# A decoder step on one core: rows of 1/rms through memory, two channel groups per matmul, and statistics moved 12 products

## The chip, the cores and the metric

The kernel runs on one core of a Trainium2 chip. A core has TensorE (PE, with its weight loads shown apart as PEld), VectorE (DVE), ScalarE (ACT), GpSimd (POOL) and SyncE (SP), which here issues nearly all DMA transfers. Matmul results land in PSUM, in banks of 512 fp32 columns. The metric is device time in microseconds, the median of several runs. Matmuls appear in the profile as passes: an fp32 product shows as two weight loads and two matmuls, a product of operands rounded to fp32r as one of each.

## The reference

One layer of a hybrid decoder, for a prompt of 1024 positions and for 8 samples of 8 new positions each (64 rows). Cut to what matters here:

```
h = RMSNorm(x)                    # x * rsqrt(mean(x*x) + eps) * gain
q, k, v, gmlp_u, gmlp_v, gate_attn, gate_gmlp = split(h @ w_in)
branch A: sliding-window attention with sinks
branch B: gelu(u) * (W_s[g] LN(gelu(v)) + b[g])  in chunks of 128 positions, 6 channel groups g,
          W_s lower-triangular; for a sample only its first 8 x 8 corner
x = x + (sigmoid(gate_a) * (A @ w_a) + sigmoid(gate_g) * (B @ w_b)) @ w_out
x = x + ConvFFN(RMSNorm(x));  final RMSNorm
```

## The kernel before, in words

The 1088 rows are worked on in two groups: group 0 has the 64 sample rows (`s`) and prompt tiles 0 to 3 (576 rows), group 1 prompt tiles 4 to 7 (512). Every large product is made of three fp32r matmuls over high and low halves of both operands (`hh`/`hl`, `w2h`/`w2l`, `wh`/`wl`), which ACT (L40) and DVE (L41) split from the raw fp32.

The first stage runs from the start to about 107 us. `tokens()` makes gmlp_v and v with the rows on the partitions: per tile of 128 rows 8 chunks of the 1024 channels, three products of 256 columns each (L555), into one PSUM bank; `gv_out` (L597) or `v_out` (L570) on ACT scales the result by the row's 1/rms and stores it. Group 0 goes first, with weights gv 0, gv 1, v, gv 2; then group 1 with v, gv 2, gv 0, gv 1, 96 products for each weight. The weights of a block have two buffers, so that those of the last block (gv 1) are split only after the block of gv 2 has freed its buffer.

1/rms is wanted in two layouts. With the rows on partitions, for the scaling above: `rsg[g]` holds the sums of squares over channel chunks, `stats_tok(g)` adds up the partitions by a matmul with a column of ones (L500) and takes root and reciprocal into `rstg[g]`, 128 partitions by one column per tile (L501, L502). And with the rows along the free dimension, the same on all partitions, for the x tiles that later products use: `stats_all(g)` spreads `rstg[g]` by matmuls with the identity (L512) into a bank, which ACT copies over `rsg[g]` (L514). `sums_of` multiplies x by it (L697). The results for group 0 are split into `t` (`t0_job`), those for group 1 are stored to memory (`t1_job`) and loaded later. These jobs run beside the products, one or none after each tile.

Then PE computes q, k, gmlp_u and the gates by a two-level scheme of seven products per pair of weights (L315, group 0 with 288 columns, group 1 with 256), from about 107 us on. Beside it the layer norm of gmlp_v is made and stored (`vnd`), and `mix_samples` at about 329 us mixes the samples' rows: for each of 6 channel groups one product of 64 rows by 64 columns (L824), with a block-diagonal 64 x 64 matrix per group (`wss`, built at L406 to L411 from a load, a mask and a predicated copy). `mix_job` does the prompt's rows (L852). Attention and the branch products follow from about 430 us, the up projection from about 790, the down projection from about 1247 us to the end.

The order of instructions on each engine is not left to a scheduler: `issue_order` walks each engine's list by a table (`ORDER`), a digit saying how many places ahead the next instruction stands. The staging ring `stg` has 4 buffers, the PSUM ring `st` 7 and `mx` one.

Of the kernel before, what the change touches and what calls it, by code (L numbers as in the profile page):

```python
# [6 lines left out]
F32 = mybir.dt.float32  # L7
F32R = mybir.dt.float32r
I32 = mybir.dt.int32
# [6 lines left out]
P = 128  # L16
D = 1024
KD = 8
NS = 64
# [5 lines left out]
NG = 6  # L25
# [9 lines left out]
def layer(tc, a):  # L35
    nc = tc.nc
    V, S, G, PE = nc.vector, nc.scalar, nc.gpsimd, nc.tensor
# [9 lines left out]
    with ExitStack() as top:  # L47
# [20 lines left out]
        ident = cst.tile([P, P], F32, name="c_ident")  # L68
# [274 lines left out]
        def pick(x, place, lo, hi):  # L343
# [5 lines left out]
                       toks=[("s", 0), *((i, NS + P * i) for i in range(4))]),  # L349
# [7 lines left out]
        dr = lambda name, shape, dt=F32: dram.tile(shape, dt, name=name)  # L357
# [5 lines left out]
        sgd = [[dr(f"sg{e}d{c}", [P, T]) for c in range(KD)] for e in range(2)]  # L363
        vd = [dr(f"vd{i}", [P, NKV, P]) for i in range(7)]
        v3d = dr("v3d", [P, 256])
        dvd = [None, *(dr(f"dvd{i}", [P, NKV, P]) for i in range(1, 8))]
        gvd = {name: dr(f"gvd{name}", [P, GW]) for gr in groups for name, _ in gr["toks"]}
        vnd = [dr(f"vnd{gr['g']}", [P, NG, len(gr["toks"]), P]) for gr in groups]
# [12 lines left out]
        with ExitStack() as ph1:  # L381
            c1 = ph1.enter_context(tc.tile_pool(name="c1", bufs=1))
# [8 lines left out]
            def stage(n):  # L391
                return stg.tile([P, 576], F32, name="stg")[:, :n]
# [3 lines left out]
            def load_late():  # L396
                nc.sync.dma_start(ident, a["ident"])
                late["mprev"] = const1("mprev", [P, 1, P], I32)
                late["sinkb"] = const1("sinkb", [P, NH])
                late["sinks"] = const1("sinks", [P, 2])  # L400
                neg = c1.tile([P, 1], F32, name="c_neg")
                V.memset(neg, NEG)
                late["neg"] = neg
                w2 = c1.tile([NS, NG, NS], F32, name="c_wss")
                w2r = stg.tile([P, 576], F32, name="stg")[:NS, :NG * NS]
                nc.sync.dma_start(w2r, a["wss"])  # L406
                m2 = stg.tile([P, 576], F32, name="stg")[:NS, :NG * NS].bitcast(I32)
                nc.sync.dma_start(m2, a["mss"])
                w2f = w2.rearrange("p a b -> p (a b)")
                V.memset(w2f, 0.0)  # L410
                V.copy_predicated(w2f, m2, w2r)  # L411
                late["wss"] = w2
# [78 lines left out]
            def bank():  # L491
                return psa.tile([P, 512], F32, name="st")

            def stats_tok(g, ps=None):
# [5 lines left out]
                    PE.matmul(pt[:, i:i + 1], acc[:, lo:lo + P], ones[:, 0:1], start=True, stop=True)  # L500
                S.activation(rstg[g], pt, AF.Sqrt, bias=eps, scale=1.0 / D)  # L501
                V.reciprocal(rstg[g], rstg[g])  # L502

            def stats_all(g):

                acc, n, toks = rsg[g], groups[g]["n"], groups[g]["toks"]
                for lo, hi in ((0, 320), (320, n)) if g == 0 else ((0, n),):
                    ps = bank()
                    for i, (name, at) in enumerate(toks):
                        m = NS if name == "s" else P  # L510
                        if lo <= at < hi:
                            PE.matmul(ps[:, at - lo:at - lo + m], rstg[g][0:m, i:i + 1].to_broadcast([m, P]),  # L512
                                      ident[0:m, 0:m], start=True, stop=True)
                    S.copy(acc[:, lo:hi], ps[:, 0:hi - lo])  # L514

            pa0, hs0o, th0, xro = ExitStack(), ExitStack(), ExitStack(), ExitStack()
            gvp = pa0.enter_context(tc.tile_pool(name="gvp", bufs=4))
# [156 lines left out]
            jobs = [x_job(k) for k in range(KD)]  # L674
            tokens(0, ("gv", 0, 1), lambda i, ps: gv_out(0, i, 1, ps), jobs, first_out)
            tokens(0, ("v", 0), lambda i, ps: v_out(0, i, ps), jobs)
            stats_all(0)
            tokens(0, ("gv", 0, 2), lambda i, ps: gv_out(0, i, 2, ps), jobs)
            hs0o.close()
            t0h, xr = right(th0, "T0h"), right(xro, "xr")  # L680
# [38 lines left out]
            none = lambda: None  # L719
            jobs = [lambda: x_in(0)] + [x for kk in range(4) for x in (t0_job(kk), none)] + [t1_job(kk) for kk in range(4)]  # L720
            tokens(1, ("v", 1), lambda i, ps: v_out(1, i, ps), jobs, lambda ps: stats_tok(1))
            stats_all(1)
            wide["again"] = True
            W.emit(W.used + 2)
            for p3 in (2, 0, 1):
# [89 lines left out]
            def mix_samples():  # L815

                mp = late["mp"]
                late["sm"] = mp.tile([P, NG, NS], F32, name="sm")
                ps = psa.tile([P, 512], F32, name="mx", bufs=1)
                for c in range(NG):  # L820
                    if c % 3 == 0:
                        v = stage(3 * P)[:NS].rearrange("p (c k) -> p c k", c=3)
                        nc.sync.dma_start(v, vnd[0][0:NS, c:c + 3, 0])
                    PE.matmul(ps[:, NS * c:NS * c + NS], v[:, c % 3], late["wss"][:, c, :], start=True, stop=True)  # L824
# [1100 lines left out]
def issue_order(tc):  # L1925
# [8 lines left out]
    for name, text in ORDER.items():  # L1934
# [20 lines left out]
        "1"  # L1955
    ),
    "Activation": (
        "1.2(4)b..91..1.44..2.11(10)1223..3(4)1..1.1...1.37..1.3..1..133.2.1(5)777cc.b..e1e.2.a3.33.22.4."
        ".39.1(5)66a.5..467(4)3.2.1.95a211..7...56(4)3..831.2.1.314..34(4)21.62..1.3.52.3.4.b.i4449.333.6"
        ".99...9..2..3.4c..li444.83.22.53.26.7..1.3.4.b.i4449.33.26.993.2.11.44..4c..4449e.f3.22.53.268(5"  # L1960
        ")3.4.7.a4.39.8.3.2.5.4..9H49.7.d47.73.7.35.7...4.2.33.7b4.711...6.1.22.44(4)2274ac2...85237221.."
        "2.37.a47.127.6.2.5.4..48..49b7.3.4.5.6...3.4.7.a47.38.74...5.4..48..49b7.3.4.5.6...3.4.6.83.b467"
        ".1.41.2.1.5346521.433..8a11.53.135.3..1..311B1(8)22(6)11.22(5)y(5)O4(5)5(5)1.44(4)1.L(4)1(7)1.1."
        "54(4)N1.44(4)1(5)1...Q(4)1.1.4(5)1.44(4)1.A(6)1(5)1(9)j1.44(5)1..q..H(6)4(5)T54(6)54(4)1.44(6)5S"
        "4(6)54(6)54(6)Q54(6)54(6)54M(6)54(6)54(6)s44..1...54(6)54c(5)1...5.61..61.2515.51.123.22.24.15.1"
        "51.14.51.152.142.24.13..45..7..1173..171.111.11(4)2...11...126.62.24.1..7..1(4)24..1(4)1.4...33."
        "..229.a.bed262..222...44..9.a.bd3...22...46...3.9.a.b3..a.922(4)5.4..9b..bd3...22...46...3.9.a.b"
        "3..a.92(5)5.4..9a..9a3...22421331..b1.3222..11.22..22.8.9bd3...2221571...3.9.a.b3..a.92211..5.4."
        ".9b..bd3...22...46...3.9.a.b3..a.92(5)5.4..9b..bd3...22...46...3.9.9.93..7.622...22..51.5325266."
        "..5(4)1e.793..a.9322...5.4..9b..bd3...22...46...3.9.a.b3..a.92(5)5.4..9b..bd3...22...46...3.9.a."  # L1970
        "b3..a.92(5)5.4..9b..bd3...22...46...3.7.7.7h...5f.1..124.34..111..41525.1(5)1(7)1.1.1.1.1.1.1.1."
        "1..1(4)KK[92]M.[90]L[89]N1MO[85]O.[83][83].[82][82].1(6)5(4)23.3.3.3.3.3.3.3.3.3.3.3.3.3.3.3.3.3"
        ".3.3(9)2j2i4.35e1466a.9.88.71(8)11121..14l13514g62.466aaaaa.91.1.1...1(5)1(5)1...1.1...1"
    ),
    "DVE": (
        "..nn2(6)91..1.44..2.1...1.1(6)123..3(4)1..1.1.1..26.1.31.2..2g.ff2.dd1ck.jj.iii...777cc.bd.c.b2a"
# [17 lines left out]
        ".77.12...11.1..3..11..11(10)21311111...88(4)4a4...a..118.111.11.111...41.1.2(5)2..3.32..1"  # L1994
    ),
    "SP": (
        "(6)1(17)6789(4)7...3.2.a.ach(10)7.e.d.3d.c.1o(5)99.aa...948..625(4)33.23f.e..511(7)1(13)21.5(4)1"
        "(4)11.3..1.OOT1S...TTVV61.1.2..1.13.2..61.1.2..1.13.2..5615...2..232622.12232vv3..vy..2.424...1."
        ".1.3..62.1.2..464.1.1.4191312.411.21.21c.1512125.1..11.11.1a1411.141...59a.8.41251.324..231...24"
        "66214..2fs1z11(5)1(18)1c.1i6p31...2.m2.63(4)2t.2.s63(4)2.m2.fd.aaab.ib.mf(9)eb(5)79.792(4)3a.d7."  # L2000
        "6g.j7.1.j1(4)1321(13)1(5)1.2...2.1.21113.52544..4..244..244..54.3.5731.8c4..1133.8K..I2...22..56"
        "..y333..1112.111l11(7)22222211..1.445221.111444455.4477...4455.4477...455.55883(4)3344...44.44.."
        ".44.66...1551.44...44.44...44.44...44.99...6(6)1...111f12..3333333..1.988...11122(41)122.111(5)1"
        ".a.9999.888l.lmn.no(24)1.1.1...1...1.1.1.1.1.1.1.1"
    ),
    "PE": (
        "(35)222222222222..223322222222..222222222222..222222222222..222222222222..222222222222(20)555555"
        "555555(3516)5555555(10)aaa(19)5(10)aaaa(52)4(176)44(175)33334(26)4(108)8833334(28)44(113)4444444"
        "444(29)4c(4)888(19)444444444(36)8(22)444444(19)88888...55544444cccc(4)8(18)dd4cccc(4)88(12)88888"
        "...444444(6)8(22)d4cccccc(4)8(12)8888...444444(7)g(8)88888888...4444cccccccccccc(4)o(8)gggggggg."  # L2010
        "..4ccckk(4)ggg(8)8888888gg...4ccccc(4)888(10)gggggggg...4cccckkkk(4)gg(8)888888gg...d4cccccc(4)8"
        "88888888888888c...9488888888888888(4)44444444.3333..111(782)666...333(2369)AAAAAAAAAA(38)cc(1210"
        ")AAAAAA(1868)22222222(36)444"
    ),
}

# [9 lines left out]
def layout(np, x_prompt, x_sample, cache_win_k, cache_win_v, state_conv, norm_mix, w_in, sinks,  # L2026
# [35 lines left out]
    ins["wss"] = np.tile(wst[:8, :, :8], (8, 1, 8)).reshape(NS, NG * NS)  # L2062
    same = (u[:, None] // 8 == u[None] // 8) & (u[:, None] % 8 <= u[None] % 8)
    ins["mss"] = np.tile(same.astype(np.int32), (1, NG))
# [43 lines left out]
```

## Time and profile before

| | us |
|---|---|
| median of 3 runs (1488.43 to 1488.82) | 1488.78 |
| the profiled execution | 1488.75 |
| its span, first to last instruction | 1486.6 |
| PE busy | 1477.0 |
| DVE busy | 1181.6 |
| ACT busy | 857.6 |
| POOL busy | 289.6 |

The profiled execution's time is 2.15 us longer than its span. In rows of a timeline the columns are the start in us from the span's beginning, the length, engine, line, operation, result<-inputs, tile shape and count, and in brackets the idle time before and what ended it. In the chain of work the columns are start, length and what ran. A wait's row gives who waited for whom, the total in us, how often, and the longest. A window's row gives its bounds and length, then the busy time of PE, PEld, DVE, ACT and POOL with counts, the granted clock, the DMA engines' share and GB/s.

### The profile page before, as it was taken

How to read it: one execution, taken by the hardware profiler on the slowest of the kernel's cores; microseconds unless marked ns; L12 is line 12 of the kernel's file. 1: busy time of each engine (PE TensorE's matmuls, PEld its weight loads, DVE VectorE, ACT ScalarE, POOL GpSimd, SP SyncE). 2: the span in 40 equal slices, each digit the busy share in tenths (PEclk: the TensorE clock that was granted, in tenths of full speed). 3: DMA queues.
4: the chain of work that ended last, by engine and by line, in shares of the span. 5: the costliest groups of instructions: out<-in, count | busy, mean ns of one | idle time of the engine just before them, and what ended most of it. 6: DMA issues, size and time to landing. Idle time of an engine off the chain costs nothing.

```text
span 1486.6 us, 30008 instructions
## 1 busy us (share of the span) xinstructions
PE 1477.0 (99%) x11454; PEld 1444.1 (97%) x11454; DVE 1181.6 (79%) x1897; ACT 857.6 (58%) x1797; POOL 289.6 (19%) x395
## 2 busy tenths in 40 slices
PE   9999999999999999999999999999999999999998
PEld 8999999999998999998989999999999999999998
DVE  7889877655587887988678898898898888785686
ACT  8657676554466775864444554654565556363463
POOL 3002110010040322310235222332242222000002
PEclk9999999999999999999999999999999999999998
DMA  7787446774779758458977433332332217983454
GB/s 250 237 290 251 166 165 221 232 233 155 239 247 320 223 158 259 135 188 306 335 268 271 131 123 119 124 124 96 118 133 96 110 59 233 345 290 102 112 164 155
DMA packets 133871, 289.24 MB, mean 195 GB/s; under 512 B 15904, under 2 KB 36064, under 8 KB 133728
## 3 DMA queue, kind: packets, MB, share of 16 engines
q1 hardware_dynamic: 133584, 287.32, 58.0%
q8 instruction: 90, 1.47, 0.4%
q14 instruction: 53, 0.43, 0.1%
q10 hardware_dynamic: 144, 0.01, 0.0%
HBM read 198.72 MB, written 90.52 MB: 195 GB/s over the span
## 4 chain that ended last, share of the span: by engine, by line
PE 95%; DVE 1%; ACT 1%; DMA 1%; issue 1%; POOL 0%; SPq 0%; POOLq 0%; DVEq 0%; ACTq 0%
PE st L315 51%; PE mm L240 17%; PE dn L1749 15%; PE st L555 6%; PE sc L1245 2%; PE po L1296 2%; PE pt L1272 1%; PE mx L852 1%; DMA wraw<-wt 0%; DMA wraw<-wpb 0%; DVE wl L41 0%; DVE s L41 0%; PE po L1196 0%; ACT four L1163 0%; POOL x L1825 0%
## 5 line engine op out<-in xcount | busy, mean ns | idle before, releaser
L315 PE MATMUL st<-t,wh 128*128 128x288 f32 x2128 | 427.7, 294 | 0.0
L315 PEld LDWEIGHTS st<-t,wh 128*128 128x128 f32 x2128 | 335.6, 188 | 0.2
L315 PE MATMUL st<-t,wl 128*128 128x288 f32 x1064 | 311.8, 293 | 0.0
L315 PE MATMUL st<-th,wh 128*128 128x256 f32 x1064 | 294.6, 277 | 0.0
L315 PE MATMUL st<-tl,wh 128*128 128x256 f32 x1064 | 294.2, 277 | 0.0
L315 PE MATMUL st<-th,wl 128*128 128x256 f32 x1064 | 293.9, 276 | 0.0
L315 PEld LDWEIGHTS st<-th,wh 128*128 128x128 f32 x1064 | 199.7, 188 | 0.2 <-ACT kn L296 0.2
L315 PEld LDWEIGHTS st<-t,wl 128*128 128x128 f32 x1064 | 199.8, 188 | 0.0
L315 PEld LDWEIGHTS st<-th,wl 128*128 128x128 f32 x1064 | 199.7, 188 | 0.0
L315 PEld LDWEIGHTS st<-tl,wh 128*128 128x128 f32 x1064 | 199.7, 188 | 0.0
L40 ACT CAST wh<-wraw 128x512 fp32r<-128x512 f32 (+2 forms) x188 | 129.2, 700 | 82.7 <-PE st L315 25.5
L1749 PE MATMUL dn<-th,wh 128*128 128x288 f32 (+1 forms) x616 | 176.6, 287 | 0.0
L1749 PE MATMUL dn<-tl,wh 128*128 128x288 f32 (+1 forms) x616 | 176.2, 286 | 0.0
L1749 PE MATMUL dn<-th,wl 128*128 128x288 f32 (+1 forms) x616 | 175.3, 285 | 0.0
L41 DVE TENSOR_TENSOR wl<-wraw,wh 128x512 fp32r<-128x512 f32 (+2 forms) x188 | 148.8, 805 | 25.2 <-ACT wh L40 23.3
L40 ACT CAST wh<-ws 128x512 fp32r<-128x512 f32 x168 | 102.7, 621 | 86.4 <-PE st L315 53.0
L41 DVE TENSOR_TENSOR wl<-ws,wh 128x512 fp32r<-128x512 f32 x168 | 117.2, 708 | 41.7 <-ACT wh L40 41.0
L1749 PEld LDWEIGHTS dn<-th,wl 128*128 128x128 f32 x616 | 115.9, 188 | 0.1
L1749 PEld LDWEIGHTS dn<-tl,wh 128*128 128x128 f32 x616 | 115.6, 188 | 0.1
L1749 PEld LDWEIGHTS dn<-th,wh 128*128 128x128 f32 x616 | 115.6, 188 | 0.1
L41 DVE TENSOR_TENSOR tl<-traw,th 128x544 fp32r<-128x544 f32 (+1 forms) x85 | 61.0, 722 | 22.6 <-ACT th L40 22.4
L40 ACT CAST th<-traw 128x544 fp32r<-128x544 f32 (+1 forms) x85 | 54.5, 643 | 40.5 <-PE dn L1749 27.0
(308 smaller groups left out, 3188.2 us busy)
## 6 DMA issues: line engine op xcount, KB each, us to landing
wraw<-wt SPq DMA_DIRECT2D x137, 512.0 KB
traw<-td SPq DMA_DIRECT2D x77, 272.0 KB
td<-za SPq DMA_DIRECT2D x22, 544.0 KB
q<-qd SPq DMA_DIRECT2D x16, 512.0 KB
upd<-hl SPq DMA_DIRECT2D x14, 512.0 KB
td<-t SPq DMA_DIRECT2D x11, 544.0 KB
wpart<-wt SPq DMA_DIRECT2D x22, 256.0 KB
qd<-q SPq DMA_DIRECT2D x8, 576.0 KB
```

Of the source, the lines that this page charges most:

```text
L40: S.copy(hi, src)
L41: V.tensor_sub(lo, src, hi.bitcast(F32))
L240: PE.matmul(ps[:, lo:lo + c1 - c0], u[:, k, :], v[:, c0:c1], start=(k == 0 and i == 0), stop=(k == nk - 1 and i == 2))
L315: PE.matmul(ps, u[:, kk, :], v, start=first and kk + i == 0, stop=kk == 3 and i == 2, skip_group_check=True)
L555: PE.matmul(ps, u, v[:, k, :], start=k + i == 0, stop=k == KD - 1 and i == len(todo) - 1)
L852: PE.matmul(ps[:, P * i:P * i + P], vn[:, i], late["wst"][:, c, :], start=True, stop=True)
L1245: PE.matmul(ps[:, h, o0:256], q, kst[kv][:, e, k0:cur + P], start=e == 0, stop=e == 1)
L1272: PE.transpose(pt[:, h * P:h * P + P], s[:, h, 0:P], ident)
L1296: PE.matmul(po, v[:, kv, :], t, start=e == 0, stop=last)
L1749: PE.matmul(place(m, e), u[:, m, :], v[:, lo:hi], start=new and i + k == 0 and (e == 0 or m % 2 == 0), stop=i == NU - 1 and k == 2, skip_g ...
```

## The change

Three edits. First, `stats_all` and its calls are gone. At the end of `stats_tok(g)` SP stores `rstg[g]` as one row of 576 or 512 numbers to memory (4-byte pieces; for group 0 the samples' 64 and the prompt's 4 x 128 apart) and loads that row back to all 128 partitions, over `rsg[g]`. Second, `wss` becomes a 128-row matrix: for each pair of channel groups a block matrix with the even group's 64 x 64 in the upper left and the odd one's in the lower right. The even groups' 64 rows of v are loaded into partitions 0 to 63 and the odd groups' into 64 to 127, and three products of 128 rows and 128 columns take the place of six of 64 and 64. The host makes the wider matrix and mask. Third, the order's table moves the second statistics; the tables of ACT and SP change with the instructions that leave or come, those of DVE and POOL do not.

```
+        rsd = [dr(f"rsd{g}", [1, n]) for g, n in ((0, 576), (1, 512))]
...
-                w2 = c1.tile([NS, NG, NS], F32, name="c_wss")
-                w2r = stg.tile([P, 576], F32, name="stg")[:NS, :NG * NS]
+                w2 = c1.tile([P, NG // 2, P], F32, name="c_wss")
+                w2r = stg.tile([P, 576], F32, name="stg")[:, :NG * NS]
...
                 V.reciprocal(rstg[g], rstg[g])
-
-            def stats_all(g):
...
+                if g == 0:
+                    nc.sync.dma_start(rsd[g][0, 0:NS], rstg[g][0:NS, 0])
+                nc.sync.dma_start(rsd[g][0, NS * (1 - g):].rearrange("(i p) -> p i", p=P), rstg[g][:, 1 - g:])
+                nc.sync.dma_start(acc, rsd[g].to_broadcast([P, groups[g]["n"]]))
...
             tokens(0, ("v", 0), lambda i, ps: v_out(0, i, ps), jobs)
-            stats_all(0)
...
             tokens(1, ("v", 1), lambda i, ps: v_out(1, i, ps), jobs, lambda ps: stats_tok(1))
-            stats_all(1)
...
-                for c in range(NG):
-                    if c % 3 == 0:
-                        v = stage(3 * P)[:NS].rearrange("p (c k) -> p c k", c=3)
-                        nc.sync.dma_start(v, vnd[0][0:NS, c:c + 3, 0])
-                    PE.matmul(ps[:, NS * c:NS * c + NS], v[:, c % 3], late["wss"][:, c, :], start=True, stop=True)
+                v = stage(3 * P).rearrange("p (c k) -> p c k", c=3)
+                for r in range(2):
+                    nc.sync.dma_start(v[NS * r:NS * r + NS], vnd[0][0:NS, r::2, 0])
+                for c in range(NG // 2):
+                    PE.matmul(ps[:, P * c:P * c + P], v[:, c], late["wss"][:, c, :], start=True, stop=True)
...
     "PE": (
...
-        "555555(3516)5555555(10)aaa(19)5(10)aaaa(52)4(176)44(175)33334(26)4(108)8833334(28)44(113)4444444"
+        "555555(337)444444444444(3155)5555555(10)aaa(19)5(10)aaaa(52)4(176)44(175)33334(26)4(108)8833334("
```

What that does to the engines' orders, at three places. The rows are in the order of issue, with result<-inputs and the shape; numbers behind names are buffers, and lines after the change are some 7 lower (L555 is L548, L500 is L501). First PE in the block of v for group 1, before: `hl_854` ends the first tile, `hh_573` (chunk 0) begins the second.

```order
L555 MATMUL st<-w2h,hh_853 128x256
L555 MATMUL st<-w2l,hh_853 128x256
L555 MATMUL st<-w2h,hl_854 128x256
L500 MATMUL mx<-c_ones,rs_251 128x1 x4
L555 MATMUL st<-w2h,hh_573 128x256
L555 MATMUL st<-w2l,hh_573 128x256
```

The same place now, from the second product of the second tile (its chunk 0 is `hh_578` and `hl_579`) to the statistics:

```order
L548 MATMUL st<-w2l,hh_578 128x256
L548 MATMUL st<-w2h,hl_579 128x256
L548 MATMUL st<-w2h,hh_614 128x256
L548 MATMUL st<-w2l,hh_614 128x256
L548 MATMUL st<-w2h,hl_615 128x256
L548 MATMUL st<-w2h,hh_651 128x256
L548 MATMUL st<-w2l,hh_651 128x256
L548 MATMUL st<-w2h,hl_652 128x256
L548 MATMUL st<-w2h,hh_688 128x256
L548 MATMUL st<-w2l,hh_688 128x256
L548 MATMUL st<-w2h,hl_689 128x256
L501 MATMUL mx<-c_ones,rs_253 128x1 x4
```

Chunks 0 to 3 of the second tile, twelve products, now stand ahead of the statistics, which have moved from the border of two tiles into the middle of one.

SP at the same time, before: transfers of x, of the stored v tile 3 (`v3d`), and of the split v (`vd`, `dvd`).

```order
L354 DMA x<-xt 128x576 x2
L586 DMA vd_146<-vst 128x512
L586 DMA dvd_153<-vst 128x512
L586 DMA vd_147<-vst 128x512
L354 DMA x<-xt 128x512
L591 DMA vp<-gv 128x256
```

And now:

```order
L354 DMA x<-xt 128x576 x2
L506 DMA rsd_151<-rst_231 128x4x1
L579 DMA vd_146<-vst 128x512
L579 DMA dvd_155<-vst 128x512
L507 DMA rs_253<-rsd_151 128x512
L579 DMA vd_147<-vst 128x512
L354 DMA x<-xt 128x512
```

The store of the second row stands ahead of two v stores, the load that reads it back behind them, ahead of another v store and of loads of x. For group 0 the two stores stand ahead of the first gv stores, and the load, 15 rows later, ahead of the first store of v.

PE at the samples' mixing, before, between products of the two-level scheme:

```order
L315 MATMUL st<-tl_1765,wh 128x256
L315 MATMUL st<-th_1764,wl 128x256
L824 MATMUL mx<-c_wss,stg 128x64 x6
L315 MATMUL st<-t_1193,wh 128x288 x2
L315 MATMUL st<-t_1193,wl 128x288
```

And now:

```order
L815 MATMUL mx<-c_wss,stg 128x128 x3
L315 MATMUL st<-t_1191,wh 128x288 x2
L315 MATMUL st<-t_1191,wl 128x288
L315 MATMUL st<-t_1192,wh 128x288 x2
L315 MATMUL st<-t_1192,wl 128x288
```

The place is the same; six products are three. The spreading (L512, five products at about 48 us and four at about 74) is simply no longer in PE's list.

More of the change, by code (lines that the diff above doesn't have):

```diff
@@ L403, in load_late @@
                 late["neg"] = neg
-                w2 = c1.tile([NS, NG, NS], F32, name="c_wss")
-                w2r = stg.tile([P, 576], F32, name="stg")[:NS, :NG * NS]
+                w2 = c1.tile([P, NG // 2, P], F32, name="c_wss")
+                w2r = stg.tile([P, 576], F32, name="stg")[:, :NG * NS]
                 nc.sync.dma_start(w2r, a["wss"])
-                m2 = stg.tile([P, 576], F32, name="stg")[:NS, :NG * NS].bitcast(I32)
+                m2 = stg.tile([P, 576], F32, name="stg")[:, :NG * NS].bitcast(I32)
                 nc.sync.dma_start(m2, a["mss"])
@@ L502, in stats_tok @@
                 V.reciprocal(rstg[g], rstg[g])
-            def stats_all(g):
[L506 to L514, printed above, removed]
+                if g == 0:
+                    nc.sync.dma_start(rsd[g][0, 0:NS], rstg[g][0:NS, 0])
+                nc.sync.dma_start(rsd[g][0, NS * (1 - g):].rearrange("(i p) -> p i", p=P), rstg[g][:, 1 - g:])
+                nc.sync.dma_start(acc, rsd[g].to_broadcast([P, groups[g]["n"]]))
             pa0, hs0o, th0, xro = ExitStack(), ExitStack(), ExitStack(), ExitStack()
@@ L1957 @@
     "Activation": (
[L1958 to L1972, printed above, removed]
@@ L1973 @@
-        ".3.3(9)2j2i4.35e1466a.9.88.71(8)11121..14l13514g62.466aaaaa.91.1.1...1(5)1(5)1...1.1...1"
+        "1.2(4)b..91..1.44..2.11(10)1223..3(4)1..1.1...1.37..1.3..1..1.2.1(5)777cc.b..d1d.2.93.3.22.4..39"
+        ".1(5)66a.5..467(4)3.2.1.95a211..7...56(4)3..831.2.1.314..34(4)21.62..1.3.52.3.4.b.i4449.333.6.99"
+        "...9..2..3.4c..li444.83.22.53.26.7..1.3.4.b.i4449.33.26.993.2.11.44..4c..4449e.f3.22.53.268(5)3."
+        "4.7.a4.39.8.3.2.5.4..9H49.7.d47.73.7.35.7...4.2.33.7b4.711...6.1.22.44(4)2274ac2...85237221..2.3"
@@ new lines @@
+        "7.a47.127.6.2.5.4..48..49b7.3.4.5.6...3.4.7.a47.38.74...5.4..48..49b7.3.4.5.6...3.4.6.83.b467.1."
+        "41.2.1.5346521.433..8a11.53.135.3..1..311B1(8)22(6)11.22(5)y(5)O4(5)5(5)1.44(4)1.L(4)1(7)1.1.54("
+        "4)N1.44(4)1(5)1...Q(4)1.1.4(5)1.44(4)1.A(6)1(5)1(9)j1.44(5)1..q..H(6)4(5)T54(6)54(4)1.44(6)5S4(6"
+        ")54(6)54(6)Q54(6)54(6)54M(6)54(6)54(6)s44..1...54(6)54c(5)1...5.61..61.2515.51.123.22.24.15.151."
+        "14.51.152.142.24.13..45..7..1173..171.111.11(4)2...11...126.62.24.1..7..1(4)24..1(4)1.4...33...2"
@@ new lines @@
+        "29.a.bed262..222...44..9.a.bd3...22...46...3.9.a.b3..a.922(4)5.4..9b..bd3...22...46...3.9.a.b3.."
+        "a.92(5)5.4..9a..9a3...22421331..b1.3222..11.22..22.8.9bd3...2221571...3.9.a.b3..a.92211..5.4..9b"
+        "..bd3...22...46...3.9.a.b3..a.92(5)5.4..9b..bd3...22...46...3.9.9.93..7.622...22..51.5325266...5"
+        "(4)1e.793..a.9322...5.4..9b..bd3...22...46...3.9.a.b3..a.92(5)5.4..9b..bd3...22...46...3.9.a.b3."
+        ".a.92(5)5.4..9b..bd3...22...46...3.7.7.7h...5f.1..124.34..111..41525.1(5)1(7)1.1.1.1.1.1.1.1.1.."
@@ L1974 @@
+        "1(4)KK[92]M.[90]L[89]N1MO[85]O.[83][83].[82][82].1(6)5(4)23.3.3.3.3.3.3.3.3.3.3.3.3.3.3.3.3.3.3."
+        "3(9)2j2i4.35e1466a.9.88.71(8)11121..14l13514g62.466aaaaa.91.1.1...1(5)1(5)1...1.1...1"
     ),
@@ L1996 @@
     "SP": (
[L1997 to L2004, printed above, removed]
+        "(6)1(17)9abc..111181114131b1bdi(11)7.g.f.3f.e.1q(5)bb2cc.11..948..625(4)33.23f.e..511(7)1(13)21."
+        "5(4)1(4)11.3..1.OOT1S...TTVV61.1.2..1.13.2..61.1.2..1.13.2..5615...2..232622.12232vv3..vy..2.424"
+        "...1..1.3..62.1.2..464.1.1.4191312.411.21.21c.1512125.1..11.11.1a1411.141...59a.8.41251.324..231"
+        "...2466214..2fs1z11(5)1(18)1c.1i6p31...2.m2.63(4)2t.2.s63(4)2.m2.fd.aaab.ib.mf(9)eb(5)79.792(4)3"
+        "a.d7.6g.j7.1.j1(4)1321(13)1(5)1.2...2.1.21113.52544..4..244..244..54.3.5731.8c4..1133.8K..I2...2"
+        "2..56..y333..1112.111l11(7)22222211..1.445221.111444455.4477...4455.4477...455.55883(4)3344...44"
+        ".44...44.66...1551.44...44.44...44.44...44.99...6(6)1...111f12..3333333..1.988...11122(41)122.11"
+        "1(5)1.a.9999.888l.lmn.no(24)1.1.1...1...1.1.1.1.1.1.1.1"
     ),
@@ L2007 @@
         "(35)222222222222..223322222222..222222222222..222222222222..222222222222..222222222222(20)555555"
-        "555555(3516)5555555(10)aaa(19)5(10)aaaa(52)4(176)44(175)33334(26)4(108)8833334(28)44(113)4444444"
[L2009 to L2013, printed above, removed]
+        "555555(337)444444444444(3155)5555555(10)aaa(19)5(10)aaaa(52)4(176)44(175)33334(26)4(108)8833334("
+        "28)44(113)4444444444(29)4c(4)888(19)444444444(36)8(22)444444(19)88888...55544444cccc(4)8(18)dd4c"
+        "ccc(4)88(12)88888...444444(6)8(22)d4cccccc(4)8(12)8888...444444(7)g(8)88888888...4444ccccccccccc"
+        "c(4)o(8)gggggggg...4ccckk(4)ggg(8)8888888gg...4ccccc(4)888(10)gggggggg...4cccckkkk(4)gg(8)888888"
+        "gg...d4cccccc(4)888888888888888c...9488888888888888(4)44444444.3333..111(782)666...333(2369)AAAA"
+        "AAAAAA(38)cc(1210)AAAAAA(1868)22222222(36)444"
     ),
@@ L2061, in layout @@
     ins["wst"] = wst
-    ins["wss"] = np.tile(wst[:8, :, :8], (8, 1, 8)).reshape(NS, NG * NS)
+    wss = np.zeros((2, NS, NG // 2, 2, NS), np.float32)
+    mss = np.zeros(wss.shape, np.int32)
     same = (u[:, None] // 8 == u[None] // 8) & (u[:, None] % 8 <= u[None] % 8)
-    ins["mss"] = np.tile(same.astype(np.int32), (1, NG))
+    for e in range(2):
+        wss[e, :, :, e] = np.tile(wst[:8, :, :8], (8, 1, 8))[:, e::2]
+        mss[e, :, :, e] = same[:, None]
+    ins["wss"], ins["mss"] = (x.reshape(P, NG * NS) for x in (wss, mss))
     ck = cache_win_k[0]
```

## The prediction

> **What bounds the kernel now.** I read the page's shares first, then who TensorE (PE) waited for, then the chain of work that ended last.
>
> ```profile
> span 1486.6 us, 30008 instructions
> PE 1477.0 (99%) x11454; PEld 1444.1 (97%) x11454; DVE 1181.6 (79%) x1897; ACT 857.6 (58%) x1797; POOL 289.6 (19%) x395
> PE 95%; DVE 1%; ACT 1%; DMA 1%; issue 1%; POOL 0%; SPq 0%; POOLq 0%; DVEq 0%; ACTq 0%
> PE sc L1146 <- issue: 1.3, 1, 1.3
> ```
>
> PE is busy 99% of the span and carries 95% of the chain; its longest wait, in attention, is 1.3 us. So a microsecond taken from PE's stream is worth a microsecond, unless the work that feeds PE cannot come earlier. The chain, in order of time (start, length, what), prices the PE work that the change touches:
>
> ```profile
> 25.43 22.35 PE st L555 x196
> 47.78 1.45 PE st L512 x10
> 49.23 15.43 PE st L555 x136
> 64.66 0.79 PE mx L500 x8
> 65.45 8.59 PE st L555 x72
> 74.03 0.89 PE st L512 x8
> 74.92 32.66 PE st L555 x288
> 107.58 221.35 PE st L315 x1788
> ```
>
> From 25 to 329 us the chain is PE's own stream, piece touching piece: nothing else is waited for there. The reader should also see a pace: 136 products in 15.43 us and 288 in 32.66 are 0.1134 us each, but the 72 between the second statistics (L500) and the second spreading (L512) take 8.59, or 0.119.
>
> **The change, part by part.** *Spreading of 1/rms by matmul removed.* The two pieces of L512 go from PE: 1.45 and 0.89 us. What follows them starts that much earlier. Sum so far 2.34. The three ACT copies behind them (L514) go too; ACT is 58% busy and no PE wait names it in this stretch, so I cost them at nothing.
>
> *The mixing of the samples.* Starts on PE's timeline around it, and around a later group of 128-row, 128-column products (L852) for comparison:
>
> ```profile
> 328.66 0.28 PE L315 MATMUL st<-th,wl 128*128 128x256 f32 x1
> 328.87 1.55 PE L824 MATMUL mx<-c_wss,stg 64*128 64x64 f32 x12
> 330.34 0.54 PE L315 MATMUL st<-t,wh 128*128 128x288 f32 x2
> 330.72 0.29 PE L315 MATMUL st<-t,wl 128*128 128x288 f32 x1
> 347.99 0.28 PE L315 MATMUL st<-th,wl 128*128 128x256 f32 x1
> 348.10 1.05 PE L852 MATMUL mx<-wst,vn 128*128 128x128 f32 x8
> 348.91 0.51 PE L315 MATMUL st<-t,wh 128*128 128x288 f32 x2
> 349.26 0.29 PE L315 MATMUL st<-t,wl 128*128 128x288 f32 x1
> ```
>
> Each fp32 product is two passes (six products, x12). From the last product before to the third after, twelve 64-row passes take 330.72 - 328.66 = 2.06 us and eight 128-row passes 349.26 - 347.99 = 1.27. Inside the groups a pass starts every (1.55 - 0.27)/11 = 0.116 us for 64 columns, (1.05 - 0.28)/7 = 0.110 for 128: the column count does not show, and going from 128 to 64 rows costs 0.1 us more at each end (328.66 to 328.87 against 347.99 to 348.10). Three products of 128 rows and columns are six passes: 1.27 - 2 x 0.11 = 1.05. Gain 2.06 - 1.05 = 1.01 us; sum 3.35. The Trainium skill has a rule that speaks against this term: in "TensorE: Matmul & The Clock Gate", section "Back-to-back issue gap", a lone warm matmul's gap is N/2.4 + 2.5 ns, so that two 64-column passes (58 ns) are worth one of 128 (56 ns) and pairing the groups gains nothing; the sum would then be 2.34. The rows above contradict it here, since both widths take 0.11 us.
>
> The two loads of v for it keep their shapes and places in SP's queue, both into one staging buffer instead of two; no use of the four-buffer ring gets closer to an earlier one. The masks' loads double, 96 to 192 KB each. Their reader on DVE stands where it did:
>
> ```profile
> 15.61 0.47 SPq L408 DMA_DIRECT2D stg<-mss  x1
> 24.35 0.58 DVE L411 COPY_PREDICATED c_wss<-stg 64x384 f32<-64x384 int32 x1
> 10.00:20.00 10.00, 9.77 (x79) 9.18 (x78) 9.64 (x14) 9.31 (x15) 9.02 (x10) 1.00 1.01 350
> ```
>
> At the 350 GB/s of that window (DMA share 1.01) 0.19 MB more is 0.55 us, in a gap of 8 us between issue and use: nothing. If it were exposed, 0.55 us.
>
> *1/rms by store and broadcast load.* No row shows a 4-byte scatter store or a broadcast load, so I bound them by when the rows exist and when they are used:
>
> ```profile
> 25.77 0.19 DVE L502 RECIPROCAL rst<-rst 128x5 f32<-128x5 f32 x1 [0.85 <-ACT rst L501]
> 53.82 0.82 DVE L697 SCALAR_TENSOR_TENSOR x<-x,c_gains,rs 128x576 f32<-128x576 f32 x1 [0.16 <-ACT rs L514]
> 67.46 0.17 DVE L502 RECIPROCAL rst<-rst 128x4 f32<-128x4 f32 x1
> 84.96 1.40 DVE L697 SCALAR_TENSOR_TENSOR x<-x,c_gains,rs 128x512 f32<-128x512 f32 x2
> SPq L1101 <- DMA msd<-stg: 18.7, 5, 8.7
> SPq L794 <- DMA vnd<-v: 7.5, 4, 2.9
> ```
>
> The first has 53.82 - 25.96 = 27.9 us, the second 84.96 - 67.63 = 17.3. A load of what the kernel itself has just stored waited at most 8.7 us on the SP queue, in another place at most 2.9. Even 8.7 for the store and as much for the load just fits 17.3. So the rows cost PE nothing directly; the cover is that slack. The indirect cost is the SP queue: the second load stands ahead of other transfers and blocks them until its store has landed.
>
> ```profile
> 68.75 0.80 SPq L354 DMA_DIRECT2D x<-xt  x2
> 70.08 0.33 SPq L586 DMA_DIRECT2D vd<-vst  x1
> 72.55 0.33 SPq L586 DMA_DIRECT2D dvd<-vst  x1
> 74.32 0.32 SPq L586 DMA_DIRECT2D vd<-vst  x1
> 78.00 0.32 SPq L586 DMA_DIRECT2D vd<-vst  x1
> 79.13 0.33 SPq L143 DMA_DIRECT2D wraw<-wt  x1
> 90.41 1.22 DVE L41 TENSOR_TENSOR w2l<-wraw,w2h 128x1024 fp32r<-128x1024 f32 x1
> ```
>
> The store goes out at 69.6, into a gap; the load comes up at 72.9 and the next vd store is ready at 74.3. With 2.9 us of landing the load leaves at once, in a gap again; with 8.7 it leaves at 78.3, and vd, x and the weight load of 79.13 come some 2 to 4 us late. ACT splits that weight ahead of the last gv weights, whose split on DVE now ends at 90.41 + 1.22 = 91.6. PE wants those 96 products before 107.58, at 96.7, and after the change at about 94.3. The cover is 2.7 us, so even the late end costs PE 0 to 1.3 us. I take zero, from the 2.9 row: its transfers lie in a window as open as this one. The two stores and the load for the first group go into SP's idle times ahead of the gv stores and of the v stores, each waiting for something that is older than what stands behind.
>
> *The second statistics 12 products later.* The same eight passes (0.79) stand elsewhere: no PE time. With L512 gone PE is 1.45 us early there and 12 x 0.1134 = 1.36 puts it back, so ACT and DVE get 1/rms when they did. What changes is the pace after them. The 72 slow products cost 8.59 - 72 x 0.1134 = 0.42, of which 0.1 is the start; some 0.3 is the slower pace. It began at L500 and ended at L512. The first statistics, 12 products into a tile, were followed by 196 products in 22.35 us, 0.114. The second stood between two tiles and now also stand 12 products in. I take the fast pace, a gain of 0.3; at the other end the slow pace holds from the statistics up to 107.58, since no L512 ends it: 60 + 288 products x 0.0042 = 1.46 us against 0.3 now, a loss of 1.2.
>
> The sum: 2.34 + 1.01 + 0.3 = 3.65 us. The profiled execution took 1488.75 us (span 1486.6 and 2.15 around it), 0.03 below the median 1488.78; 1488.75 - 3.65 = 1485.1.
>
> **Does it reach the end?** PE's one large wait and the pieces off PE on the chain lie between 429 and 463 us:
>
> ```profile
> 426.93 0.62 ACT L40 CAST wh<-ws 128x512 fp32r<-128x512 f32 x1 [0.50 <-PE st L315]
> 429.48 1.21 DVE s L41
> 445.67 5.76 DMA wraw<-wpb
> 430.00:435.00 5.00, 5.00 (x46) 5.00 (x45) 5.00 (x9) 4.28 (x9) 1.52 (x3) 1.00 0.94 327
> ```
>
> There DVE is busy 5.00 of 5 us and the DMA engines 0.94. If that work ran by its own time, PE would arrive early and wait. But ACT still waits for PE at 426.93, and the chain enters DVE at 429.48 from PE, so the stretch starts when PE gets there and should move with it.
>
> **The rivals.** (1) *Slow pace.* All savings come, but the 348 products run at 0.1176: 2.34 + 1.01 - 1.2 = 2.15 gained, 1486.6. For it: one of the two statistics did start it, and it holds until something breaks it. Against: the one in the new position did not. (2) *Swallowed at 429 to 463.* DVE and the loads there do not move, and PE's wait of 1.3 us grows by up to 3.4: 1488.4 at worst, within 0.2%. Against: the two rows that tie it to PE. (3) *The pairing gains nothing*: a pass costs by its columns, so that six passes of 128 take what twelve of 64 took; gain 2.34 + 0.3, 1486.1. The 0.116 against 0.110 us speaks against it. (This is the skill's rule above.) (4) *Slower: the SP queue.* The second load waits for its store and holds up the weight loads. PE is late by what the landing takes beyond 72.9 - 69.6 = 3.3 us, SP's 0.8 us of room before 79.13 (78.32 to 79.13) and PE's 2.7: it eats the 3.65 only if the store needs more than about 10.4 us, and with 14 us, the price 7.2, the time is 1492.3. The longest wait of this sort is 8.7. Nothing else in the change adds work to PE. That a product order does not do what it says is excluded: the rows of the order show all four edits.
>
> **How the numbers follow.** A measurement here tells 0.2%, or 2.98 us, from no change: below 1485.8 is faster. Forecast 0.55, of which one part in ten lands above 1485.8 (its own range 1484.3 to 1486.0, from the 0.3 us of pace, the 0.55 of the masks and the 0.4 by which runs of the kernel before differ). Slow pace 0.22, one part in seven below 1485.8. Swallowed 0.14. Pairing 0.03. SP queue or another late transfer 0.06. Faster 0.5 + 0.03 = 0.53, slower 0.06, same 0.41. The range from 1484.3 to 1487.4 holds the forecast, rival 1, rival 3 and the lesser half of rival 2, 0.8 in all.
>
> **What would show it.** Right: no matmul of c_ident into st before 110 us, the L315 stretch beginning near 104.9 instead of 107.58; six passes in the mixing, about 0.7 us long; pieces of the gv products at 0.1134 each after the second statistics; the SP rows of the two rs loads with nothing on DVE waiting for them. The lead after the mixing, about 3.6, is still there at 470. Wrong: 0.1176 per product from 66 to 105; a PE wait for w2l near 94; a PE wait at L1146 above 3 us; SP idle before the second rs load for more than 5 us.

## The result and the profile after

The changed kernel is slower: 1498.37 us median of six runs (1495.49 to 1499.37) against 1488.94 of the kernel before beside it, a ratio of 1.0061 (95% interval 1.0051 to 1.0071; the ratios here are estimates over the runs, not quotients of two medians). The forecast was 1485.1, with a range up to 1487.4. The profiled execution took 1499.21, its span 10.4 us more than before.

The page, its chain shares, and who PE waited for, of the kernel after:

```profile
span 1497.0 us, 29968 instructions
PE 1477.6 (99%) x11430; PEld 1444.6 (97%) x11430; DVE 1180.1 (79%) x1897; ACT 855.5 (57%) x1794; POOL 291.4 (19%) x395
PE 93%; DMA 2%; ACT 2%; DVE 1%; issue 1%; POOL 0%; SPq 0%; POOLq 0%; ACTq 0%; DVEq 0%
PE st L548 <- ACT w2h L40: 7.1, 1, 7.1
PE st L548 <- DVE w2l L41: 3.1, 2, 2.1
```

PE is still "99% busy", which shows how little that figure says: new waits of together 10.2 us stand in the first stage, where the kernel before had none of that kind. L548 is the old L555. Pieces of the chain, first for the stretch in which those waits arise, then as the counterpart to the rows of before (start, length, what):

```profile
27.35 11.11 DMA gvd<-gv
...
78.74 10.16 DMA vd<-vst
...
93.56 1.15 DVE w2l L41
94.75 24.53 PE st L548 x191
119.28 221.35 PE st L315 x1788
340.64 0.67 PE mx L815 x6
341.30 17.64 PE st L315 x144
358.94 0.89 PE mx L843 x8
```

From 25 to 107 us the chain had been PE alone. Now two transfers of 11.11 and 10.16 us stand on it, a gv store and a vd store, and L315 begins at 119.28 instead of 107.58. The timeline shows what was sent just ahead of those two, and who waited (brackets: idle before, and what ended it):

```profile
26.38 0.57 SPq L506 DMA_DIRECT2D rsd<-rst  x1
27.35 1.79 SPq L593 DMA_DIRECT2D gvd<-gv  x4
38.54 0.92 ACT L590 ACTIVATE gv<-gs,rst 64x256 f32<-64x256 f32 x2 [7.69 <-DMA gvd<-gv]
...
77.47 0.43 SPq L506 DMA_DIRECT2D rsd<-rst  x1
78.74 0.33 SPq L579 DMA_DIRECT2D vd<-vst  x1
87.51 0.32 SPq L507 DMA_DIRECT2D rs<-rsd  x1
88.98 0.40 ACT L40 CAST vst<-gv 128x256 fp32r<-128x256 f32 x1 [7.93 <-DMA vd<-vst]
92.10 0.58 PE L548 MATMUL st<-w2h,hh 128*128 128x256 f32 x1 [7.12 <-ACT w2h L40]
```

In both places the 4-byte stores are followed by some 10 us in which the transfer behind them does not land. ACT stands at a `gv` or `vst` buffer whose store has not landed, 7.69 and 7.93 us. Of the first wait 1.0 us reaches PE, at 49.68 us (3.1 less 2.1 of the `w2l` row). In the second, the casts of the next block's weights (gv 0, at 91.01 and 92.30 us) stand behind the waiting cast in ACT's queue, so PE starves for `w2h` and `w2l`. Windows, the kernel before first (28:36 and 80:88), then after; the last three columns are the granted clock, the DMA engines' share, and GB/s:

```profile
28.00:36.00 8.00, 8.00 (x73) 8.00 (x72) 7.46 (x16) 7.46 (x17) 0.00 (x0) 1.00 0.72 212
80.00:88.00 8.00, 8.00 (x73) 8.00 (x72) 7.26 (x14) 5.67 (x11) 0.00 (x0) 1.00 0.91 308
```

```profile
28.00:36.00 8.00, 8.00 (x73) 8.00 (x72) 3.10 (x7) 2.82 (x7) 0.00 (x0) 1.00 1.18 60
80.00:88.00 8.00, 4.98 (x43) 4.77 (x41) 2.62 (x8) 0.93 (x3) 0.00 (x0) 1.00 0.62 62
95.00:98.00 3.00, 3.00 (x15) 3.00 (x16) 2.61 (x6) 2.29 (x6) 0.00 (x0) 0.50 0.84 228
98.00:100.00 2.00, 2.00 (x11) 2.00 (x11) 2.00 (x6) 0.80 (x3) 0.00 (x0) 0.50 1.03 401
100.00:105.00 5.00, 5.00 (x45) 5.00 (x44) 5.00 (x8) 4.43 (x8) 0.00 (x0) 0.97 0.90 303
```

From 28 to 36 us the DMA engines are shown busier than before (1.18 against 0.72) and move 60 GB/s instead of 212. I read a busy share beside so few bytes as packets that are in flight and do not finish; no row shows single packets. The last three rows are the price of the stall itself: by windows of 1 us the granted clock fell from 1.00 to 0.55 between 90 and 91 us, 5 us into the wait, and PE then ran at 0.50 up to about 100 us; the 191 products behind the stall took 24.53 us where 191 x 0.1134 is 21.66, 2.9 more.

So the loss adds up as: waits 10.2, half clock 2.9, a slower pace ahead of the stall 0.4 (157 products at 4.2 ns more, less the 0.3 us that before had lost so; the pace is below), less 2.34 of spreading, is 11.2 of the 11.7 us by which L315 is late; for the other 0.5 I have no row. The pairing then gives 1.0 back (358.94 - 119.28 = 239.66 us from L315's start to the first L843; before, 348.26 - 107.58 = 240.68), and the span ends 10.4 later. The end of that stretch in the kernel before:

```profile
330.41 17.85 PE st L315 x144
348.26 0.89 PE mx L852 x8
```

### The profile page after: what moved, and what is told of

The parts are those of the page before. It is cut to its first block, busy times and chain, and to the rows that moved or that the text cites. A ratio compares the mean times of both kernels' runs of the same rounds, so it can differ in the third digit from the quotient of the medians.

```text
span 1497.0 us, 29968 instructions
## 1 busy us (share of the span) xinstructions
PE 1477.6 (99%) x11430; PEld 1444.6 (97%) x11430; DVE 1180.1 (79%) x1897; ACT 855.5 (57%) x1794; POOL 291.4 (19%) x395
## 4 chain that ended last, share of the span: by engine, by line
PE 93%; DMA 2%; ACT 2%; DVE 1%; issue 1%; POOL 0%; SPq 0%; POOLq 0%; ACTq 0%; DVEq 0%
PE st L315 52%; PE mm L240 16%; PE dn L1740 15%; PE st L548 4%; PE sc L1236 2%; PE po L1287 2%; PE pt L1263 1%; DMA gvd<-gv 1%; PE mx L843 1%; DMA vd<-vst 1%; DMA wraw<-wt 0%; PE po L1187 0%; ACT four L1154 0%; DMA x<-xt 0%; DMA stg<-xt 0%
## 5 line engine op out<-in xcount | busy, mean ns | idle before, releaser
L315 PE MATMUL st<-t,wh 128*128 128x288 f32 x2128 | 427.6, 294 | 0.0
L315 PEld LDWEIGHTS st<-t,wh 128*128 128x128 f32 x2128 | 335.5, 188 | 0.1
L315 PE MATMUL st<-t,wl 128*128 128x288 f32 x1064 | 311.8, 293 | 0.0
L315 PE MATMUL st<-th,wh 128*128 128x256 f32 x1064 | 294.6, 277 | 0.0
L315 PE MATMUL st<-tl,wh 128*128 128x256 f32 x1064 | 294.2, 277 | 0.0
L315 PE MATMUL st<-th,wl 128*128 128x256 f32 x1064 | 293.9, 276 | 0.0
L315 PEld LDWEIGHTS st<-th,wh 128*128 128x128 f32 x1064 | 199.8, 188 | 0.2 <-ACT kn L296 0.2
L315 PEld LDWEIGHTS st<-t,wl 128*128 128x128 f32 x1064 | 199.8, 188 | 0.0
L315 PEld LDWEIGHTS st<-th,wl 128*128 128x128 f32 x1064 | 199.7, 188 | 0.0
L315 PEld LDWEIGHTS st<-tl,wh 128*128 128x128 f32 x1064 | 199.7, 188 | 0.0
```

The source lines that it names most:

```text
L315: PE.matmul(ps, u[:, kk, :], v, start=first and kk + i == 0, stop=kk == 3 and i == 2, skip_group_check=True)
```

## The experiments

**One part at a time.** e1 is the kernel before with the rows edit alone, e2 the changed kernel without it, e3 the pairing alone, e4 the second statistics' move alone. The order's tables follow in each. The kernel before was run again beside them; its medians were 1488.77 for e1 to e4, 1488.36 for e5 to e8 and 1488.52 for e9 to e12.

```
e1:  -stats_all(g) and its calls   + the three stores and two loads of the change
e2:  the changed kernel            + stats_all(g), - the stores and loads
e3:  -6 products 64 x 64 (L824)    + 3 products of 128 x 128, wider wss
e4:  PE's table: the four products of the second statistics 12 places later
```

> The kernel before with the rows of 1/rms by store and broadcast load alone; pairing and the moved statistics are left out. Theory A (the 4-byte stores hold up the transfers behind them on the DMA queue for about 10 us, twice, and ACT waits for a buffer whose store stands behind them): it carries the whole loss, 1498 to 1501 us, some 1 us above the changed kernel because the mixing still costs 2.06; PE waits in front of the gv products as there, 8 to 10 us in all. Theory B (the loss comes from the doubled mask loads or from the place of the second statistics): about 1486.6, the 2.34 us of L512 gained and nothing lost.

> The changed kernel with the spreading by matmul put back in place of the store and load; pairing and moved statistics stay. Theory A: 1487.6 to 1488.0, that is 1.0 us below before and nothing else moved. Theory B: 1498 or so, as the changed kernel.

> The kernel before with the mixing of two channel groups per matmul alone. Prediction's term: 1.0 us faster, 1487.9. Rival of the prediction (a pass goes by its columns): no change, 1488.9. If the doubled mask loads delay the first weights: slower than 1488.9.

> The kernel before with the second statistics 12 products later alone; L512 still stands after the block. If the place between two tiles brought the slow pace of 0.1176 us: the 60 products left run at 0.1134 and it is 0.3 us faster, 1488.6. If the slow pace follows the statistics wherever they stand (as the changed kernel's trace suggests): 60 slow products instead of 72, 0.05 us, no change.

| | median us | runs | ratio to before (95%) |
|---|---|---|---|
| e1 rows only | 1498.37 | 4 | 1.0068 (1.0054 to 1.0082) |
| e2 all but rows | 1488.06 | 11 | 0.9996 (0.9987 to 1.0005) |
| e3 pairing only | 1487.28 | 11 | 0.9995 (0.9986 to 1.0004) |
| e4 statistics only | 1488.31 | 11 | 1.0002 (0.9993 to 1.0011) |

The rows edit carries the whole loss; PE's waits for `w2h` and `w2l` are in e1 as well (6.1 and 2.9 us). The other two edits cannot be told from nothing in the time. In the trace of e4 the products behind the moved statistics are still slow (281 ns each at 68 to 74 us), so the place of the statistics does not choose the pace. And the trace can tell the pairing. Chain of e3:

```profile
107.09 221.35 PE st L315 x1788
328.44 0.67 PE mx L824 x6
329.11 17.64 PE st L315 x144
346.75 0.89 PE mx L852 x8
```

From the start of L315 to the first L852 it is 346.75 - 107.09 = 239.66 us again: 1.02 less than before, as in the kernel after.

**Which part of the rows edit?** The theory (A): a scattered store of 4-byte pieces keeps other transfers from landing for about 10 us. Its rival, the fourth of the prediction: SP stands at the second load, which must wait for its store. SP did wait there for 5.9 us in the kernel after. e5 stores the rows and never loads them; the spreading by matmul stays. e6 and e9 change the addresses alone, e7 the pieces, e10 the queue.

```
e5:  + the three stores of the change, in their places; no load
e6:  rsd [1, n] -> [n, 128], element i to rsd[i, 0]      (512 bytes apart)
e9:  rsd [1, n] -> [n, 16],  element i to rsd[i, 0]      (64 bytes apart)
e7:  nc.sync.dma_start(rsd[g], rstg[g])                  (128 pieces of 20 or 16 bytes)
e10: as e5, nc.sync -> nc.scalar                         (ACT's queue)
```

> The kernel before, with the three 4-byte stores added at the places that they have in the changed kernel; nothing loads the rows, and the spreading by matmul stays. Theory A (each scattered store occupies the way to memory for about 10 us, and the gv and vd stores behind it hold ACT's buffers): the loss of the rows edit without its 2.34 us gain, 1488.8 + 9.6 + 2.3, so 1499 to 1502, with PE waits for w2h and w2l near 92 us of 5 us and more. Rival 4 of the prediction (SP stands at the second load, and the weight loads behind it are late): there is no load, so 1488.8 within 1 us and no PE wait above 1.5 us.

> As e5, but each element is stored into a row of its own, 512 bytes apart. If the 10 us come from many 4-byte writes into the same lines of memory, it falls to 1488.8 to 1492. If they come from the number of pieces, whatever their addresses, it stays at e5's time within 2 us.

> As e5, but rstg is stored as it lies: 128 pieces of 20 bytes, later 128 of 16, instead of 576 and 512 of 4. If the price is by the piece, 128/576 of 10 us is 2.2 us per store, inside the room of 3.3 + 0.8 + 2.7 us: 1488.8 to 1490. If any store of small pieces blocks for 10 us, as e5.

> As e6, with the elements 64 bytes apart instead of 512. If what costs is several writes into one piece of memory of 64 bytes or less, it stays with e6: 1488 to 1489.5 and no PE wait above 1.5 us. If the unit in which writes collide is larger (256 or 512 bytes), part or all of the loss of e5 is back: 1491 to 1501.

> As e5 (same three 4-byte stores, nothing loads the rows), but issued from ACT's queue instead of SP's. If the gv and vd stores are late because they stand behind the scattered store in one queue, the loss goes: 1488 to 1490, gvd<-gv lands as in the kernel before. If the memory or the 16 DMA engines as such are taken up, it stays: 1498 to 1501, with ACT's wait of about 7 us for gvd<-gv and PE's for w2h and w2l.

| | median us | runs | ratio to before (95%) |
|---|---|---|---|
| e5 stores only | 1499.98 | 4 | 1.0072 (1.0057 to 1.0088) |
| e6 512 bytes apart | 1489.02 | 10 | 1.0003 (0.9994 to 1.0012) |
| e9 64 bytes apart | 1488.49 | 10 | 1.0000 (0.9991 to 1.0009) |
| e7 as they lie | 1488.70 | 10 | 1.0003 (0.9994 to 1.0012) |
| e10 ACT's queue | 1501.72 | 4 | 1.0093 (1.0078 to 1.0109) |

Waits and the first window of e5, where nobody ever reads the rows:

```profile
ACT gv L602 <- DMA gvd<-gv: 6.9, 1, 6.9
PE st L560 <- ACT w2h L40: 5.2, 1, 5.2
28.00:36.00 8.00, 8.00 (x73) 8.00 (x72) 3.04 (x7) 2.77 (x7) 0.00 (x0) 1.00 1.09 66
```

The same window in e6, then in e9, then in e10:

```profile
28.00:36.00 8.00, 8.00 (x73) 8.00 (x72) 7.46 (x16) 7.46 (x17) 0.00 (x0) 1.00 0.76 216
```

```profile
28.00:36.00 8.00, 8.00 (x73) 8.00 (x72) 7.46 (x17) 7.46 (x18) 0.00 (x0) 1.00 0.77 210
```

```profile
28.00:36.00 8.00, 8.00 (x73) 8.00 (x73) 3.23 (x7) 2.96 (x7) 0.00 (x0) 1.00 1.20 58
```

e5 falsifies rival 4: without any load the loss is all there, and as large as theory A said. e6 and e9 narrow A down. The same 576 and 512 writes of 4 bytes, from the same places in SP's queue, cost nothing when they lie 64 or 512 bytes apart: 210 to 216 GB/s move where 66 did. The profile counts the same 135007 DMA packets in e5, e6 and e9, 1136 more than before, so spreading the addresses did not merge or split the writes. So it is neither the number of pieces nor their size, but many small writes close together. Distances between 4 and 64 bytes were not tried, so whether sharing 64 bytes is what counts, or a smaller unit, or lying within 2 KB as a whole, stays open. e7 has fewer and larger pieces, three or four to 64 bytes, and costs nothing that can be measured; it does not say whether the count or the crowding spared it. e10 settles the queue: from ACT's queue the stores hold up the gv stores in SP's just as well (58 GB/s; the chain has `gvd<-gv` at 9.50 us and `vd<-vst` at 9.87; the median is 0.7 us above the expected range). Order within a queue is not the cause, and ACT's queue no remedy.

The Trainium skill bears on this in "DMA: Bandwidth & Descriptors", section "Specifications": below 512 bytes a transfer is a read-modify-write. All the stores of e5, e6 and e9 are below it, and only e5 is slow, so the rule as it stands does not tell them apart. That the read-modify-writes of neighbours wait for each other would fit, but no run here shows it.

**The way around it.** In e8 one product against `c_ident` per group turns `rstg` into rows, ACT copies them, and the store writes contiguous pieces; the broadcast loads and all places in SP's queue stay. In e11 the second group's product is issued four times. In e12 the first group's rows are turned like that, with the two stores behind the first four gv stores in SP's queue and not ahead of them; the second group keeps its spreading, and of the other edits only the pairing is in.

```
e8:  + PE.matmul(ps[0:m, 384:512], rstg[g], ident)    10 products after the statistics
     + S.copy(acc[0:m, 0:P], ps[0:m, 384:512])
       store from acc[.., 0:P]: 1 x 64 and 4 x 128 numbers, in place of rstg[g]
e11: e8, the second group's product x 4, 16 products after its statistics
e12: before + pairing; e8's rows for g == 0; stats_all(1) stays; the statistics not moved
```

> The changed kernel, with the 1/rms turned by one product against c_ident per group, copied by ACT, and stored as 1 + 4 and 4 contiguous pieces (64 x 4 and 128 x 4 bytes); the broadcast loads and all places in SP's queue stay. Theory A: the loss goes, and what is left are the gains of the prediction less two small products (2 x 0.25 us): 1485.3 to 1487. If the broadcast load or SP's wait at it carries part of the loss, over 1490, with PE waits for w2h or w2l near 92 us.

> As e8, with the second group's turning product issued four times over (eight passes, as many as the spreading had; 0.66 us more PE work) 16 products after the statistics, where PE needn't wait for the reciprocal (0.4 us less). Theory P: a group of eight passes of another shape flips the pace of the products after it, as L500 and L512 did in the kernel before: the products after it take 0.1134 us, and the L315 stretch begins at 107.50 - 1.4 - 0.4 + 0.66 = 106.4 against 107.50 in e8. Rival: it takes the spreading's own kind of product (128 columns of a broadcast, into a bank of its own) to end the slow pace: 0.1176 up to the L315 stretch, which begins at 107.8. The time moves by 1 us at most: 1488 to 1490 either way.

> The kernel before, with the pairing and with the first group's rows turned by one product, stored in 1 + 4 pieces behind the gv stores and loaded by broadcast; the second group keeps its spreading by matmul, and the statistics stand where they stood. The first spreading's 1.45 us go, the turning product costs 0.25 to 0.35, the pairing brings 1.0, and the pace is that of the kernel before: the L315 stretch begins 1.1 us earlier than in the kernel before and the end comes 2.1 earlier, 1486.2 (1485.5 to 1487.2). If the gains are given back further down, as in e8, 1488 to 1489.

| | median us | runs | ratio to before (95%) |
|---|---|---|---|
| e8 turned rows | 1489.57 | 11 | 1.0007 (0.9998 to 1.0016) |
| e11 eight passes | 1488.19 | 10 | 0.9999 (0.9990 to 1.0008) |
| e12 first group only | 1486.37 | 11 | 0.9987 (0.9978 to 0.9996) |

e8 removes the loss, but the forecast gain does not come: 1489.57 against the 1485.3 to 1487 expected. From its chain and, with the bracket, its timeline:

```profile
28.97 3.09 DMA gvd<-gv
40.84 3.83 DMA rs<-rsd
66.98 0.38 PE L505 MATMUL mx<-c_ident,rst 128*4 128x128 f32 x2 [0.38 <-DVE rst L503]
67.36 40.13 PE st L552 x339
107.50 221.36 PE st L315 x1788
```

The gv store lands in 3.09 us instead of 11.11, and the broadcast load, which no row of before had shown, takes 3.83. But 339 products take 40.13 us, or 0.1184 each. The pace shows best in the mean length of one product (last number but one, in ns). Rows of the groups by shape, first of e5 at 53 to 65, 67 to 75 and 77 to 87 us, then of e8 and e11 at 72 to 100:

```profile
L560 PE MATMUL st<-w2l,h 128*128 128x256 f32 x29 | 8.1, 281 | 0.0
...
L560 PE MATMUL st<-w2l,hh 128*128 128x256 f32 x23 | 6.3, 276 | 0.0
...
L560 PE MATMUL st<-w2l,hh 128*128 128x256 f32 x29 | 8.1, 281 | 0.0
```

```profile
L552 PE MATMUL st<-w2l,hh 128*128 128x256 f32 x80 | 22.5, 281 | 0.0
```

```profile
L554 PE MATMUL st<-w2l,hh 128*128 128x256 f32 x83 | 22.9, 276 | 0.0
```

In e5 the pace was slow ahead of the second statistics (no row says why), fast behind them and slow again behind the spreading: either group of eight passes flips it, in both directions. In the kernel before they had made it slow and fast again; where the second group is gone, it stays slow. In e11 eight passes made it fast, as theory P said. But the product also had to wait 1.68 us for the reciprocal (its place was chosen 16 products behind, and DVE was late). In the changed kernel the slow pace ended over a stall, with no such group in between (281 ns at 68 to 84 us, 276 at 101 to 118), so e11 does not tell the passes from the wait. Its L315 stretch began at 108.00: theory P's 106.4 with the wait of 1.68 added is 108.1, and it is near the rival's 107.8 only because of that wait. So in these traces the second group's spreading, 0.89 us of PE, paid for itself: the pace was fast behind it, and the slow one would have cost 1.2 us.

e12 draws that conclusion. Chain of e12 (L562 are the products, L505 the turning, L519 the second spreading):

```profile
23.96 1.00 PE st L501 x9
24.96 1.13 PE st L562 x9
26.10 0.32 PE st L505 x2
26.41 36.82 PE st L562 x323
...
64.02 8.59 PE st L562 x72
72.61 0.89 PE st L519 x8
73.50 32.66 PE st L562 x288
106.16 221.35 PE st L315 x1788
...
328.18 17.64 PE st L315 x144
```

From 24 to 328 us the chain is PE alone again, the 72 products at the slow pace take the 8.59 us that they took before, and the median is 1486.37 where 1486.2 was expected. It is faster than both kernels by medians, and than the one before by its interval, though by 0.13%, less than the 0.2% that the prediction took as the limit. From the end of the first statistics to L315 it is 81.20 us against 107.58 - 25.43 = 82.15.

## Why the prediction was wrong

- *What bounds the kernel, and that PE's time counts one to one*: right. e12 took 0.95 us from the first stage and 1.02 from the mixing and is some 2 us faster.
- *Spreading removed, 2.34 us*: right as PE's work (1.45 became 0.32 in e12). That it went unseen is the doing of the next two points.
- *1/rms by store and load, no cost*: **the step that failed.** "The rows cost PE nothing directly" held: nothing waited long for the rows. The cost came from what the step did not ask: what the store does to other transfers. The prediction bounded the landing of a 4-byte scatter by the landing of large stores (2.9 and 8.7 us) and charged its lateness only to SP's queue at the second load. The second load did leave 10.0 us after its store (77.47 to 87.51), but by the sum of rival 4 that makes PE 3.2 us late (10.0 less 6.8 of room), less than the 3.65 gained: hardly faster, but not slower, and e5 has the whole loss without the load. What was missing is that the gv and vd stores do not land meanwhile, from whatever queue, that ACT waits for their buffers, and that PE's weights stand behind ACT. The two stores for the first group were put "into SP's idle times" at no price; they idled ACT for 7.69 us. Work that this delayed also made the second store late: it left at 77.47, where the prediction had 69.6 and e6, whose stores block nothing, has 70.8.
- *A stall costs more than its length*: not in the prediction at all. The half clock behind it added 2.9 us. The Trainium skill, "TensorE: Matmul & The Clock Gate", section on the HAM clock gate, has the clock halved after an idle window of about 3.4 us, until about as long a busy one. This trace agrees with the first (the clock halved 5 us into a wait of 7.12 us); for the second it shows between 5 and 6 us, from 94.75, when PE is fed again, to a little past 100, which fits a window that this page of the Trainium skill calls free-running.
- *The pace after the second statistics*: the fast end was taken, and it was the slow one, in the kernel after up to its stall and in e8 up to the L315 stretch. The choice rested on one event, the first statistics, inside a tile; but those are ten passes and not eight, and behind either of the first group's two sets of ten the pace of the kernel before is fast (276 ns at 27 to 46 and at 50 to 64 us). Rival 1 had the right reading: no L512, no end of the slow pace. As a size this term is small, 1.5 us between its two ends.
- *The pairing, 1.01 us*: right, 1.02 by e3's chain. Rival 3, which would have made it nothing (64 and 128 columns costing by width), is contradicted. The formula that the prediction cites beside this term is for a lone matmul; these passes run in a stream of weight loads and matmuls.
- *429 to 463 us*: right. e12's lead of 330.41 - 328.18 = 2.2 us at the mixing is still there at the end, in a span of 1483.9 against 1486.6, and PE's wait in that stretch is 1.0 us against 1.3.

Open remain what in the memory or the DMA engines makes neighbouring writes slow; the cause of the two paces; whether crowding or number spared e7; and 2 us of e8: its profiled execution (1487.52) was the fastest of eleven, so its rows do not explain the median of 1489.57.

## What to carry to other kernels

Look at where the pieces of a small store go, not only at its bytes and its waiter: 2 KB written as 4-byte neighbours kept other transfers from landing for some 10 us, and moving it to ACT's queue did not help; writing contiguous rows, or giving each number its own 64 bytes, did. When an operation has no row in the profile, ask what it does to the other transfers under way, and who waits for their buffers, before it is priced by its own reader. And a stall of PE like the one here, of 7 us, is to be charged with the slow clock behind it.

## What the hardware showed unexpectedly

Beside writes of 4 bytes side by side all traffic came to 58 to 66 GB/s, while the DMA engines were shown at 1.09 to 1.20 of their time; with the same writes 64 bytes apart it was 210. Products of 256 columns have two paces, 276 and 281 ns long (one every 0.1134 or 0.1176 us), and behind a group of eight short passes the pace had switched, in either direction; behind ten it had not.
